# Down projection of a SwiGLU block: pairs of column blocks, seven block products for a third of the k-tile pairs

## The chip, the cores and the metric

The program runs on one core of one Trainium2 chip. The metric is the device time of one execution in microseconds (us), median over runs. The trace comes from one profiled execution of the same program; its time is 1664.86 us and its span 1663.1 us.

TensorE (PE, with its weight load PEld), VectorE (DVE), ScalarE (ACT) and GpSimd (POOL) each work through a queue of their own, in order. Weights come from HBM by DMA, issued from SyncE's queue (SP).

## The reference

One layer of a decoder trunk on 256 tokens of width 2048, in float32: a mixer of three branches, then

```python
h = h + mixed @ w_out
hn = rmsnorm(h, norm_ffn_g)
h = h + (silu(hn @ ffn_w_gate) * (hn @ ffn_w_up)) @ ffn_w_down     # 2048 -> 5632 -> 2048
hp = rmsnorm(h, norm_ple_g)
h = h + (p @ ple_w_proj) * sigmoid(hp @ ple_w_gate)
```

and a final RMSNorm. This case is about the last product of the SwiGLU line, the down projection: (256 x 5632) times (5632 x 2048), added to h.

## The kernel before, in words

**Numbers.** A float32 operand is split into a high part of reduced precision (`hi`, made on ACT by a cast) and the rest (`lo`, made on DVE by a subtraction). One product of a 128 x 128 block of activations (stationary) with a 128 x 512 block of weights (moving) is then three matmuls, hi·hi, lo·hi and hi·lo: `mm2` issues the first two for part 0 and the third for part 1 (L139 to L145).

**Weights.** All weights lie in one array of chunks of 128 x 2048 floats, 1 MB each, in the order of their use. `load` (L102) issues the DMA of a chunk into one of three `raw` tiles; `chunk` (L113) splits it in two steps of 128 x 1024, each into a `whi` and a `wlo` tile out of a ring of three. `split` (L190) does the same for any tile: the cast on ACT is L193, the subtraction on DVE L194.

**Gate and up.** For each of 11 blocks of 512 hidden columns (L1251) the gate and the up product run together over eight pairs of k-tiles, in the order `ORDER`. Five of the pairs use eight block products (two token tiles, two k-tiles, two weight matrices), which is 24 matmuls. The three pairs in `SEVEN` use seven: sums of activation blocks (`SF`, made once, L1212) and sums of weight blocks (`seven`, L1232: two subtractions or additions on DVE, two on POOL at L1240 and L1244, into `tsum`) take part, and the seven products go to four PSUM banks of the pool `mm` (products 2, 4, 3 and 8) and four of the pool `sm` (products 1, 7, 5 and 6, which only these pairs use). After the last such pair the four `sm` banks are combined into four tiles of the pool `b2`, on ACT (`m1`, L1284) and DVE (`u2`, `u3`, `u4`, `v4`); at the end of the block the four `mm` banks are added to them (L219 is the line of the helper `tt`). A gated product `sg` follows (L222, L225), and eight transposes on PE (L1306, into `sm` banks) bring it into `hid`, 44 k-tiles of 128 x 256 (L1307).

**Down.** For each of four blocks of 512 output columns (L1316) `gemm_tm` (L156) runs over the 44 k-tiles, four to a chunk: two token tiles, so eight block products and 24 matmuls to a chunk, accumulated in two of the four `mm` banks. For every chunk the four k-tiles of `hid` are split into `dh` and `dl` in one step of 128 x 1024, so that the whole of `hid` is split four times. The result is added to the residual tiles `h[t, n]` (L1319), and `h_block` (L1157) squares them on ACT, transposes them on PE (L1167, eight transposes into two `sm` banks) and splits the transposes on ACT and DVE (L196, L197, four steps of 128 x 256) as the input of the next product, the PLE gate.

**Order of work.** The program is written in one order, and a scheduler with priorities places the instructions on the engines' queues and gives the buffers of the pools to tiles; once placed, each queue runs in order. Loads, splits of weights and of `hid`, and the combinations at the end of a gate and up block stand in `tc.high_priority()`. The pools have 4 buffers (`mm`, `sm`), 16 (`b2`), 3 (`raw`, `whi`, `wlo`) and 2 (`dh`, `dl`, `tsum`).

Of the kernel before, what the change touches and what calls it, by code (L numbers as in the profile page):

```python
# [38 lines left out]
SEVEN = (0, 1, 2)  # L39

# [34 lines left out]
def trunk(ctx: ExitStack, tc: tile.TileContext, xT, x, pT, wall, vecs, csts, s5b, s5c, gfin, out, dbg=None):  # L75
# [114 lines left out]
    def split(hi, lo, src, gain=None):  # L190
# [4 lines left out]
        else:  # L195
            nc.scalar.activation(out=hi, in_=src, func=AF.Identity if not isinstance(gain, float) else AF.Copy, scale=gain)  # L196
            nc.vector.scalar_tensor_tensor(out=lo, in0=src, scalar=gain, in1=hi.bitcast(F32), op0=ALU.mult, op1=ALU.subtract)  # L197

# [1001 lines left out]
    dn = hid_stack.enter_context(tc.tile_pool(name="dn", bufs=2))  # L1200
# [4 lines left out]

    SF = {}  # L1212
    for u in SEVEN:
        af = t2("af").rearrange("p (a t) -> p a t", a=2)
        sf = t2("sf").rearrange("p (a t) -> p a t", a=4)
        tt(af, hh[:, 2 * u:2 * u + 2, :].bitcast(F32), hl[:, 2 * u:2 * u + 2, :].bitcast(F32), ALU.add)
        tt(sf[:, 0], af[:, 0, TS[1]], af[:, 1, TS[1]], ALU.add)
        tt(sf[:, 1], sf[:, 0], af[:, 0, TS[0]], ALU.subtract)
        tt(sf[:, 2], af[:, 0, TS[0]], af[:, 0, TS[1]], ALU.subtract)
        tt(sf[:, 3], af[:, 1, TS[0]], sf[:, 1], ALU.subtract)  # L1220
        SF[u] = tuple(gu.tile([128, 4, 128], F32R, name=q + "%d" % u) for q in ("sh", "sl"))
        split(*SF[u], sf)

    def tiled(r):

        n = r.shape[1]
        hi = ring.tile([128, 2, 512], F32R, name="whi", tag="whi", bufs=3)[:, 0:n]
        lo = ring.tile([128, 2, 512], F32R, name="wlo", tag="wlo", bufs=3)[:, 0:n]
        split(hi, lo, r)
        return [(hi[:, q], lo[:, q]) for q in range(n)]  # L1230

    def seven():  # L1232

        if not loaded:
            load()
        raw, _ = loaded.pop(0)
# [11 lines left out]
    def A(u, t, k):  # L1248
        return hh[:, 2 * u + k, TS[t]], hl[:, 2 * u + k, TS[t]]

    for b in range(11):  # L1251
        M = {q: pmm() for q in (2, 4, 3, 8)}
        done = set()

        def prods(ops, last):
# [249 lines left out]
```

## Time and profile before

| | |
|---|---|
| time, median of 3 runs | 1666.72 us (1664.29 to 1666.83) |
| the profiled execution | 1664.86 us |
| its span | 1663.1 us, 23487 instructions |
| PE busy | 1641.0 us, 99% of the span |
| DVE busy | 1276.8 us, 77% |
| ACT busy | 908.7 us, 55% |
| POOL busy | 184.8 us, 11% |
| DMA | 313.69 MB, mean 189 GB/s |

Busy times are sums over instructions. Matmuls are pipelined and their ends are modelled, so PE's share says that PE is always occupied, not at what rate; that is read from the starts of its instructions. A wait is booked to what released it. The down projection lies between 1310.1 and 1553.2 us, gate and up between 837 and 1310 us.

### The profile page before, as it was taken

The page shows a single profiled execution, that of the slowest core. Times are in us where ns is not written, and L with a number is a line of the kernel's source. Part 1 is how long each engine was busy: PE and PEld are TensorE (multiplying, and loading weights), DVE is VectorE, ACT ScalarE, POOL GpSimd, SP SyncE. Part 2 cuts the span into 40 slices and gives each one's busy share as a digit, 9 for nine tenths or more (in the row PEclk, how much of TensorE's full clock was granted, in tenths as well). Part 3 has the DMA queues.
Part 4 walks back from the last instruction along what each step waited for, and adds up shares of the span by engine and source line. Part 5 has one row for each costly group of instructions (what it writes and reads, how often), then busy time and mean ns, then how long its engine had stood idle before and what let it go on. Part 6 is the DMA issues. An engine that isn't in the chain of part 4 may idle for free.

```text
span 1663.1 us, 23487 instructions
## 1 busy us (share of the span) xinstructions
PE 1641.0 (99%) x9255; PEld 1380.4 (83%) x9255; DVE 1276.8 (77%) x1590; ACT 908.7 (55%) x1141; POOL 184.8 (11%) x131
## 2 busy tenths in 40 slices
PE   8999999999999999999999999999999999999997
PEld 8999889987888888888877888888888888888886
DVE  6999776969988545575589988888888867666565
ACT  6465566555645434444465555555555656656454
POOL 1100100100000000000032322332233000000000
PEclk9999999999999999999999999999999999999999
DMA  9655544555454444555544555555555655555553
GB/s 363 196 171 175 171 152 183 189 187 190 164 194 159 149 158 152 178 190 194 213 176 181 190 198 203 202 203 192 189 190 190 232 184 197 180 200 185 219 186 118
DMA packets 49455, 313.69 MB, mean 189 GB/s; under 512 B 5824, under 2 KB 9152, under 8 KB 12736
## 3 DMA queue, kind: packets, MB, share of 16 engines
q1 hardware_dynamic: 43488, 304.59, 50.7%
q0 software_dynamic: 3840, 3.15, 1.1%
q10 hardware_dynamic: 2016, 4.46, 0.8%
q8 instruction: 72, 1.18, 0.3%
q14 instruction: 39, 0.32, 0.1%
HBM read 306.93 MB, written 2.10 MB: 186 GB/s over the span
## 4 chain that ended last, share of the span: by engine, by line
PE 94%; DVE 3%; issue 1%; ACT 1%; DMA 1%; POOL 0%; SPq 0%; POOLq 0%; DVEq 0%
PE mm L142 23%; PE mm L143 23%; PE mm L145 23%; PE mm L149 4%; PE mm L152 4%; PE mm L150 4%; PE M L145 2%; PE M L142 2%; PE M L143 2%; DVE wlo L129 1%; DMA raw<-in_wall 1%; PE sm L544 1%; DVE wlo L194 1%; PE sm L1306 0%; PE mm L135 0%
## 5 line engine op out<-in xcount | busy, mean ns | idle before, releaser
L128 ACT CAST whi<-raw 128x1024 fp32r<-128x1024 f32 (+1 forms) x496 | 518.1, 1049 | 552.5 <-PE mm L143 393.4
L129 DVE TENSOR_TENSOR wlo<-raw,whi 128x1024 fp32r<-128x1024 f32 (+1 forms) x496 | 612.2, 1238 | 240.2 <-ACT whi L128 221.4
L143 PE MATMUL mm<-whi,alo 128*128 128x512 f32 x512 | 201.2, 393 | 0.0
L142 PE MATMUL mm<-whi,ahi 128*128 128x512 f32 x512 | 201.0, 393 | 0.0
L142 PE MATMUL mm<-whi,hhi 128*128 128x512 f32 x506 | 198.1, 392 | 0.3 <-DVE m1s L219 0.3
L143 PE MATMUL mm<-whi,hlo 128*128 128x512 f32 x506 | 196.8, 389 | 0.0
L149 PE MATMUL mm<-ahi,whi 128*128 128x256 f32 x576 | 143.3, 286 | 7.8 <-ACT whi L128 7.8
L145 PE MATMUL mm<-wlo,hhi 128*128 128x512 f32 x506 | 146.5, 393 | 0.8 <-DVE wlo L194 0.8
L150 PE MATMUL mm<-alo,whi 128*128 128x256 f32 x576 | 142.7, 285 | 0.0
L145 PE MATMUL mm<-wlo,ahi 128*128 128x512 f32 x512 | 139.2, 392 | 0.0
L142 PE MATMUL mm<-whi,dh 128*128 128x512 f32 x352 | 130.2, 389 | 0.0
L143 PE MATMUL mm<-whi,dl 128*128 128x512 f32 x352 | 130.2, 389 | 0.0
L149 PEld LDWEIGHTS mm<-ahi,whi 128*128 128x128 f32 x576 | 111.4, 194 | 8.8 <-ACT whi L128 8.0
L145 PEld LDWEIGHTS mm<-wlo,hhi 128*128 128x128 f32 x506 | 94.9, 188 | 24.0 <-DVE wlo L194 4.7
L142 PEld LDWEIGHTS mm<-whi,hhi 128*128 128x128 f32 x506 | 95.0, 188 | 23.1 <-issue 3.8
L142 PEld LDWEIGHTS mm<-whi,ahi 128*128 128x128 f32 x512 | 96.1, 188 | 21.2 <-issue 1.2
L143 PEld LDWEIGHTS mm<-whi,alo 128*128 128x128 f32 x512 | 96.1, 188 | 20.9 <-issue 1.2
L145 PEld LDWEIGHTS mm<-wlo,ahi 128*128 128x128 f32 x512 | 95.6, 188 | 20.6 <-issue 0.4
L150 PEld LDWEIGHTS mm<-alo,whi 128*128 128x128 f32 x576 | 111.4, 194 | 0.4 <-issue 0.4
L143 PEld LDWEIGHTS mm<-whi,hlo 128*128 128x128 f32 x506 | 95.0, 188 | 19.6
L1244 POOL TENSOR_TENSOR tsum<-raw,tsum 128x512 f32<-128x512 f32 x33 | 86.8, 2629 | 115.6 <-DVE tsum L219 110.4
L1240 POOL TENSOR_TENSOR tsum<-raw 128x512 f32<-128x512 f32 x33 | 56.0, 1696 | 381.9 <-PE mm L145 177.5
(536 smaller groups left out, 2842.0 us busy)
## 6 DMA issues: line engine op xcount, KB each, us to landing
raw<-in_wall SPq DMA_DIRECT2D x283, 1024.0 KB, 4.8
xrow<-in_x SPq DMA_DIRECT2D x2, 1024.0 KB, 8.7
h<-in_x ACTq DMA_DIRECT2D x8, 256.0 KB, 3.2
xraw<-in_xT SPq DMA_DIRECT2D x3, 512.0 KB, 10.7
ub<-Bh POOLq DMA_DIRECT2D x16, 64.0 KB, 3.8
ub<-uh POOLq DMA_DIRECT2D x16, 64.0 KB, 3.7
gft<-in_gfin ACTq DMA_DIRECT2D x1, 1024.0 KB, 6.0
out_dram<-fin SPq DMA_DIRECT2D x4, 256.0 KB, 3.2
```

The lines of the kernel that those rows point to most:

```text
L128: nc.scalar.copy(out=hi[:, q, :], in_=r)
L129: nc.vector.tensor_tensor(out=lo[:, q, :], in0=r, in1=hi[:, q, :].bitcast(F32), op=ALU.subtract)
L142: nc.tensor.matmul(ps, ah, wh, start=first, stop=False, skip_group_check=skip)
L143: nc.tensor.matmul(ps, al, wh, start=False, stop=False, skip_group_check=skip)
L145: nc.tensor.matmul(ps, ah, wl, start=False, stop=last, skip_group_check=skip)
L149: nc.tensor.matmul(ps, wh, ah, start=first, stop=False, skip_group_check=skip)
L150: nc.tensor.matmul(ps, wh, al, start=False, stop=False, skip_group_check=skip)
L152: nc.tensor.matmul(ps, wl, ah, start=False, stop=last, skip_group_check=skip)
L194: nc.vector.tensor_tensor(out=lo, in0=src, in1=hi.bitcast(F32), op=ALU.subtract)
L544: nc.tensor.matmul(psy[32 * j:32 * j + 32, a * 256:(a + 1) * 256], cc[:, ri, js_, :], G["s5x"][q][ri][:, a, :], start=ri == 0, stop=ri == ...
L1240: nc.gpsimd.tensor_tensor(out=ts_[:, 0], in0=raw[:, 3], in1=raw[:, 0], op=ALU.subtract)
L1244: nc.gpsimd.tensor_tensor(out=ts_[:, 2], in0=raw[:, 1], in1=ts_[:, 1], op=ALU.subtract)
```

## The change

The gate and up loop becomes a function `gemm_pair` that also serves the down projection. There it runs twice, for column blocks 0 and 1 and for 2 and 3, over 22 pairs of k-tiles in their order. A plain pair is one chunk of 24 matmuls as before, now with two k-tiles and two column blocks in it. Seven of the 22 pairs (1, 4, 7, 10, 13, 16, 19) go by seven block products. `hid` is split per pair of k-tiles, in steps of 128 x 512, once for each of the two passes; in the seven pairs four sums of 128 x 128 blocks of `hid` are made on DVE and split as well, in each pass. `dh` and `dl` have three buffers, `dsh` and `dsl` two. After pair 19 the combinations of the `sm` banks are added to the four `h` tiles, and after pair 21 the `mm` banks. Both `h_block`s of a pass follow it. The weight chunks are laid out on the host to fit; their number and size stay. Gate and up computes what it did.

```diff
+DORDER = tuple(range(22))
+DSEVEN = (1, 4, 7, 10, 13, 16, 19)
...
-    def gemm_tm(hi, lo, nkt, split_of=None):
+    def gemm_tm(hi, lo, nkt):
...
-            if split_of is not None:
-                with tc.high_priority():
-                    h_, l_ = (dn.tile([128, 4, T], F32R, name=q, tag=q) for q in ("dh", "dl"))
-                    split(h_, l_, split_of[:, 4 * c:4 * c + 4, :])
-                hi, lo = (lambda k: h_[:, k % 4, :]), (lambda k: l_[:, k % 4, :])
...
+    def sums(sf, a):
+        tt(sf[:, 0], a[:, 0, TS[1]], a[:, 1, TS[1]], ALU.add)
+        tt(sf[:, 1], sf[:, 0], a[:, 0, TS[0]], ALU.subtract)
+        tt(sf[:, 2], a[:, 0, TS[0]], a[:, 0, TS[1]], ALU.subtract)
+        tt(sf[:, 3], a[:, 1, TS[0]], sf[:, 1], ALU.subtract)
...
+    def gemm_pair(A, S, order, by7, pool, prep=None, onto=None):
+        M = {q: pmm() for q in (2, 4, 3, 8)}
...
+        for u in order:
+            last = u == order[-1]
+            if prep is not None:
+                prep(u)
+            if u in by7:
+                if u == by7[0]:
+                    for q in (1, 7, 5, 6):
+                        M[q] = psm("M%d" % q)
+                (b11, b21), (b22, t3), (t1, t2_), (t4_,) = seven(pool)
+                end = u == by7[-1]
+                prods([(1, A(u, 0, 0), b11)], end)
+                prods([(2, A(u, 0, 1), b21)], last)
+                prods([(3, S(u, 3), b22)], last)
+                prods([(7, S(u, 2), t3)], end)
+                prods([(5, S(u, 0), t1)], end)
+                prods([(6, S(u, 1), t2_)], end)
+                prods([(4, A(u, 1, 1), t4_)], last)
+                if end:
+                    with tc.high_priority():
+                        m1, u2, u3, u4, v4 = (t2(q) for q in ("m1s", "u2", "u3", "u4", "v4"))
+                        nc.scalar.copy(out=m1, in_=M[1])
...
+                    res = (m1, u3, u4, v4)
+                    if onto is not None:
+                        for o, r in zip(onto, res):
+                            tt(o, o, r, ALU.add)
+                        res = onto
+            else:
+                b11, b21, b22, b12 = chunk()
+                prods([(2, A(u, 0, 0), b11), (4, A(u, 1, 0), b11), (2, A(u, 0, 1), b21), (4, A(u, 1, 1), b21)], last)
+                prods([(3, A(u, 0, 0), b12), (8, A(u, 1, 0), b12), (3, A(u, 0, 1), b22), (8, A(u, 1, 1), b22)], last)
+        with tc.high_priority():
+            for o, q in zip(res, (2, 4, 3, 8)):
+                tt(o, M[q], o, ALU.add)
+        return res
...
-    dn = hid_stack.enter_context(tc.tile_pool(name="dn", bufs=2))
+    dn = hid_stack.enter_context(tc.tile_pool(name="dn", bufs=3))
...
-    for n in range(4):
-        ps = gemm_tm(None, None, 44, split_of=hid)
-        for t in range(2):
-            nc.vector.tensor_tensor(out=h[t, n], in0=h[t, n], in1=ps[t], op=ALU.add)
-        h_block(n, hT2, "gple", ssq2)
+    dv = {}
+    def down_prep(u):
+        a = hid[:, 2 * u:2 * u + 2, :]
+        with tc.high_priority():
+            dv["a"] = tuple(dn.tile([128, 2, T], F32R, name=q, tag=q) for q in ("dh", "dl"))
+            split(*dv["a"], a)
+            if u in DSEVEN:
+                sf = t2("sf").rearrange("p (a t) -> p a t", a=4)
+                sums(sf, a)
+                dv["s"] = tuple(dn.tile([128, 4, 128], F32R, name=q, tag=q, bufs=2) for q in ("dsh", "dsl"))
+                split(*dv["s"], sf)
+    for n in (0, 2):
+        gemm_pair(lambda u, t, k: tuple(q[:, k, TS[t]] for q in dv["a"]), lambda u, i: tuple(q[:, i, :] for q in dv["s"]),
+                  DORDER, DSEVEN, hid_p, down_prep, (h[0, n], h[1, n], h[0, n + 1], h[1, n + 1]))
+        for m in (n, n + 1):
+            h_block(m, hT2, "gple", ssq2)
```

## Rows read from the trace of the kernel before

**Rows 1.** The page: busy time by engine, the chain that ended last by engine, and the group that counts the down projection's matmuls of one of the three kinds.

```profile
PE 1641.0 (99%) x9255; PEld 1380.4 (83%) x9255; DVE 1276.8 (77%) x1590; ACT 908.7 (55%) x1141; POOL 184.8 (11%) x131
...
PE 94%; DVE 3%; issue 1%; ACT 1%; DMA 1%; POOL 0%; SPq 0%; POOLq 0%; DVEq 0%
...
L142 PE MATMUL mm<-whi,dh 128*128 128x512 f32 x352 | 130.2, 389 | 0.0
```

**Rows 2.** Busy time by stretch: the second block of gate and up, one in the middle of the stage, and the whole of the down projection. Columns: stretch, its length, busy us (instructions) of PE, PEld, DVE, ACT and POOL, granted clock, DMA share, GB/s.

```profile
880.50:924.50 44.00, 43.11 (x191) 34.55 (x190) 41.38 (x43) 25.25 (x30) 10.72 (x6) 1.00 0.53 192
...
1181.20:1224.10 42.90, 42.90 (x193) 34.95 (x191) 37.61 (x41) 24.44 (x30) 13.15 (x6) 1.00 0.54 195
1310.10:1553.20 243.10, 243.10 (x1089) 201.37 (x1088) 169.13 (x157) 143.50 (x162) 0.00 (x0) 1.00 0.54 193
```

**Rows 3.** PE in order of time (start, length): two steps of one chunk in the down projection, each of which ends with four matmuls of part 1.

```profile
1364.63 1.07 PE L145 MATMUL mm<-wlo,dh 128*128 128x512 f32 x4
...
1367.35 1.07 PE L145 MATMUL mm<-wlo,dh 128*128 128x512 f32 x4
```

**Rows 4.** The chain in order of time (start, length): the transposes of two successive column blocks.

```profile
1376.58 0.66 PE sm L1167 x6
...
1437.36 0.66 PE sm L1167 x6
```

**Rows 5.** PE's waits (total us, times, longest): all of the down projection, then the second block of gate and up, then the steady block from 1138.33 us, which the later ones repeat.

```profile
PEld mm L142 <- issue: 0.3, 1, 0.3
...
PEld mm L145 <- DVE wlo L194: 1.4, 2, 0.7
PEld mm L142 <- issue: 0.5, 1, 0.5
PEld M L145 <- DVE wlo L194: 0.3, 1, 0.3
PEld sm L1306 <- DVE sg L222: 0.2, 1, 0.2
...
PEld mm L145 <- DVE wlo L194: 0.4, 1, 0.4
```

**Rows 6.** DVE in order of time in gate and up and at its start: a split of 128 x 1024, a 128 x 512 sum and the next split back to back, and two sums of 128 x 128.

```profile
908.38 1.22 DVE L129 TENSOR_TENSOR wlo<-raw,whi 128x1024 fp32r<-128x1024 f32 x1
909.51 0.69 DVE L219 TENSOR_TENSOR tsum<-raw 128x512 f32<-128x512 f32 x1
910.12 1.22 DVE L129 TENSOR_TENSOR wlo<-raw,whi 128x1024 fp32r<-128x1024 f32 x1
...
842.04 0.48 DVE L219 TENSOR_TENSOR sf<-af 128x128 f32<-128x128 f32 x2
```

**Rows 7.** DVE by shape over seven steady blocks of gate and up, 1010 to 1310 us, 21 pairs by seven products: busy us, mean ns, idle before and its releaser. The last row is the same split over the down projection, where POOL does nothing.

```profile
L129 DVE TENSOR_TENSOR wlo<-raw,whi 128x1024 fp32r<-128x1024 f32 x71 | 93.6, 1327 | 0.0
L194 DVE TENSOR_TENSOR wlo<-raw,whi 128x1024 fp32r<-128x1024 f32 x42 | 57.1, 1399 | 0.0
L194 DVE TENSOR_TENSOR wlo<-tsum,whi 128x1024 fp32r<-128x1024 f32 x21 | 28.2, 1343 | 16.2 <-PE mm L145 16.2
L219 DVE TENSOR_TENSOR raw<-raw 128x512 f32<-128x512 f32 x21 | 14.5, 690 | 16.7 <-POOL tsum L1240 16.7
...
L129 DVE TENSOR_TENSOR wlo<-raw,whi 128x1024 fp32r<-128x1024 f32 x89 | 108.9, 1224 | 64.4 <-ACT whi L128 63.8 <-ACT hid L1307 0.5
```

**Rows 8.** POOL's two sums in a steady block of gate and up (start, length).

```profile
1097.05 1.30 POOL L1240 TENSOR_TENSOR tsum<-raw 128x512 f32<-128x512 f32 x1 [12.93 <-DMA raw<-in_wall]
...
1107.88 2.28 POOL L1240 TENSOR_TENSOR tsum<-raw 128x512 f32<-128x512 f32 x1
1111.69 1.68 POOL L1244 TENSOR_TENSOR tsum<-raw,tsum 128x512 f32<-128x512 f32 x1 [1.53 <-DVE tsum L219]
```

**Rows 9.** ACT by shape over the same seven blocks, and a cast of 128 x 1024 of `hid` over the down projection.

```profile
L193 ACT CAST whi<-tsum 128x1024 fp32r<-128x1024 f32 x21 | 22.1, 1054 | 39.8 <-PE mm L143 39.8
L193 ACT CAST whi<-tsum 128x512 fp32r<-128x512 f32 x21 | 12.9, 615 | 0.7
...
L193 ACT CAST dh<-hid 128x1024 fp32r<-128x1024 f32 x42 | 44.2, 1052 | 0.0
```

**Rows 10.** The boundary between two blocks of gate and up, in order of time: the first of the final additions that wait for the old block's last banks, the last gated product, the transposes, the copies that free their banks, and the first matmul into a bank of `sm`. The new block's matmuls begin at 1267.24 us.

```profile
1268.15 1.28 DVE L219 TENSOR_TENSOR u<-mm,u 128x512 f32<-128x512 f32 x2
...
1275.28 0.74 DVE L222 SCALAR_TENSOR_TENSOR sg<-v,rr,sg 128x512 f32<-128x512 f32 x1
...
1278.69 0.60 PE L1306 MATMUL sm<-ct,sg 128*128 128x128 f32 x4
...
1279.90 1.20 ACT L1307 COPY hid<-sm 128x256 f32<-128x256 f32 x4 [1.20 <-PE sm L1306]
...
1280.49 0.40 PE L142 MATMUL M<-whi,hhi 128*128 128x512 f32 x1
```

**Rows 11.** The boundary between two column blocks of the down projection: the additions to `h`, the first and the last of the four splits of the transposes.

```profile
1370.95 1.28 DVE L1319 TENSOR_TENSOR h<-h,mm 128x512 f32<-128x512 f32 x2 [1.09 <-PE mm L145]
...
1377.46 0.48 DVE L197 SCALAR_TENSOR_TENSOR plo<-sm,vt,phi 128x256 fp32r<-128x256 f32 x1 [1.75 <-ACT phi L196]
...
1382.04 0.48 DVE L197 SCALAR_TENSOR_TENSOR plo<-sm,vt,phi 128x256 fp32r<-128x256 f32 x1
```

**Rows 12.** The end of the down projection: the first matmul of the PLE gate, and the last split of the transposes of column block 3.

```profile
1553.69 0.50 PE L142 MATMUL mm<-whi,phi 128*128 128x512 f32 x1 [0.23 <-ACT whi L128]
...
1564.50 0.48 DVE L197 SCALAR_TENSOR_TENSOR plo<-sm,vt,phi 128x256 fp32r<-128x256 f32 x1
```

More of the change, by code (lines that the diff above doesn't have):

```diff
@@ new lines, in tiled, with seven @@
+    def tiled(r):
+        n = r.shape[1]
+        hi = ring.tile([128, 2, 512], F32R, name="whi", tag="whi", bufs=3)[:, 0:n]
+        lo = ring.tile([128, 2, 512], F32R, name="wlo", tag="wlo", bufs=3)[:, 0:n]
+        split(hi, lo, r)
+        return [(hi[:, q], lo[:, q]) for q in range(n)]
+    def seven(pool):
+        if not loaded:
+            load()
+        raw, _ = loaded.pop(0)
+        with tc.high_priority():
+            ts_ = pool.tile([128, 3, 512], F32, name="tsum", tag="tsum", bufs=2)
+            out_ = [tiled(raw[:, 0:2])]
+            nc.gpsimd.tensor_tensor(out=ts_[:, 0], in0=raw[:, 3], in1=raw[:, 0], op=ALU.subtract)
+            tt(raw[:, 3], raw[:, 2], raw[:, 3], ALU.subtract)
+            out_.append(tiled(raw[:, 2:4]))
+            tt(ts_[:, 1], raw[:, 3], raw[:, 0], ALU.add)
+            nc.gpsimd.tensor_tensor(out=ts_[:, 2], in0=raw[:, 1], in1=ts_[:, 1], op=ALU.subtract)
+            out_ += [tiled(ts_[:, 0:2]), tiled(ts_[:, 2:3])]
+        return out_
@@ new lines, in gemm_pair, with prods @@
+    def gemm_pair(A, S, order, by7, pool, prep=None, onto=None):
+        M = {q: pmm() for q in (2, 4, 3, 8)}
+        done = set()
+        def prods(ops, last):
+            n_ = {q: max(i for i, o in enumerate(ops) if o[0] == q) for q in {o[0] for o in ops}}
+            for part in range(2):
+                for i, (q, a, w) in enumerate(ops):
+                    mm2(M[q], *a, *w, part, q not in done, last and part == 1 and i == n_[q], True)
+                    if part == 0:
+                        done.add(q)
+        for u in order:
[19 more added lines that the diff above has]
+                        nc.scalar.copy(out=m1, in_=M[1])
+                        tt(u2, M[6], m1, ALU.add)
+                        tt(u3, M[7], u2, ALU.add)
+                        tt(u4, M[5], u2, ALU.add)
+                        tt(v4, M[5], u3, ALU.add)
+                    res = (m1, u3, u4, v4)
[11 more added lines that the diff above has]
+        return res
@@ L1203, in trunk @@
     hh, hl = hT
[L1212 to L1236, printed above, removed]
-        with tc.high_priority():
-            ts_ = gu.tile([128, 3, 512], F32, name="tsum", tag="tsum", bufs=2)
-            out_ = [tiled(raw[:, 0:2])]
-            nc.gpsimd.tensor_tensor(out=ts_[:, 0], in0=raw[:, 3], in1=raw[:, 0], op=ALU.subtract)
-            tt(raw[:, 3], raw[:, 2], raw[:, 3], ALU.subtract)
-            out_.append(tiled(raw[:, 2:4]))
-            tt(ts_[:, 1], raw[:, 3], raw[:, 0], ALU.add)
-            nc.gpsimd.tensor_tensor(out=ts_[:, 2], in0=raw[:, 1], in1=ts_[:, 1], op=ALU.subtract)
-            out_ += [tiled(ts_[:, 0:2]), tiled(ts_[:, 2:3])]
-        return out_
+    SF = {u: sums_of(hh, hl, u, gu) for u in SEVEN}
     def A(u, t, k):
@@ L1251, in trunk @@
     for b in range(11):
[L1252 to L1295 removed]
+        c11, c21, c12, c22 = gemm_pair(A, lambda u, i: tuple(q[:, i, :] for q in SF[u]), ORDER, SEVEN, hid_p)
         sg = []
[L1297 removed]
+        for t, (g_, u_) in enumerate(((c11, c12), (c21, c22))):
             s_ = t2("sg")
```

59 lines of the change are left out of this document (17 added, 42 removed).

## The prediction

> **What bounds the kernel now.** I read the page first. PE is busy for 99% of the span and holds 94% of the chain that ended last, at the full clock [rows 1, 2]: time is gained where PE has less to issue, and lost where it has to wait. Then the table by stretches, since a mean over the run hides that the down projection is unlike its neighbour: there PE is busy in all of its 243.1 us, DVE in 169.1 (70%), ACT in 143.5 (59%), POOL not at all [rows 2]. Then PE's starts, because its lengths are modelled. Two like steps of 12 matmuls start 1367.35 - 1364.63 = 2.72 us apart, so one costs 0.2267 us [rows 3]. Three kinds of 352 are 1056 matmuls [rows 1], 239.4 us. From one column block to the next are 1437.36 - 1376.58 = 60.78 us [rows 4], less 264 x 0.2267 = 59.84: 0.94 us for eight transposes. 239.4 + 4 x 0.94 = 243.2 is the whole stage, so PE loses nothing there; its only wait in the list is 0.3 us [rows 5].
>
> Gate and up already works as the down projection will. Its steady block takes 42.9 us for 183 matmuls (41.5) and eight transposes (0.94): about 0.45 us are lost, and the list names a wait of 0.4 us for a `wlo` of DVE [rows 2, 5]. Its second block, where DVE is busy in 41.4 of 44 us (94%) in place of 37.6 of 42.9 (88%), loses 2.4 us by its four waits [rows 2, 5].
>
> **The matmuls.** Each of the seven pairs issues 21 matmuls in place of 24. Two passes of seven: 42 matmuls less, 42 x 0.2267 = 9.5 us, all on the path. PE's work becomes 507 x 0.2267 + 1.9 = 116.8 us in a pass, 233.6 in both.
>
> On this rate a page of the Trainium skill, "TensorE: Matmul & The Clock Gate" (Part 1), gives 215.7 ns for a warm matmul of 512 columns. The trace disagrees, with 226.7 ns [rows 3]; by the page the saving would be 9.1 us.
>
> **DVE.** From one start to the next a split of 128 x 1024 takes 1.13 us, an operation of 128 x 512 0.61, one of 128 x 128 0.20 [rows 6]; a split of a transpose 0.48 [rows 11]. A plain pair costs two weight splits and one of `hid` half as large as before: 2 x 1.13 + 0.61 = 2.87. A pair by seven: three large weight splits and a small one, 4.00; two sums for `seven`, 1.22; `dl`, 0.61; four small sums, 0.80; `dsl`, 0.61; together 7.24, against 21 x 0.2267 = 4.76 of PE. A pass has 15 x 2.87 = 43.1, 7 x 7.24 = 50.7, 12 combinations and additions to `h`, 7.3, and eight splits of transposes, 3.8: 104.9 us, beside 116.8 of PE. That leaves 11.9, or 1.70 us to each pair by seven for what POOL does to DVE.
>
> The trace shows two such costs. In 21 pairs by seven the 134 large splits take 93.6 + 57.1 + 28.2 = 178.9 us, where 1.224 each (POOL idle) would be 164.0: 14.9 more, 0.71 a pair. And DVE waits 16.7 us for POOL's first sum, 0.80 a pair [rows 7]. With the first DVE comes to 109.9 of 116.8 (94%), with both to 115.5 (99%). So PE remains the bound, barely, and the deficit of a pair by seven, 7.24 + 0.71 - 4.76 = 3.2 us, must be covered by what lies ready: the ring of three holds two steps ahead, 5.4 us of PE in a plain pair, and the two plain pairs that follow give back 2 x (5.44 - 2.87) = 5.1. Covered, with little over.
>
> What PE loses is bounded by the steady block (0.4 us to three pairs by seven, 0.13 each) and the second (2.4, 0.8 each) [rows 5]: 1.9 to 11.2 us over 14 pairs. Nothing below zero, as PE has no idle time to give. DVE's share is that of the second block, but pairs by seven are three apart here and mostly two there, so twice the recovery; I take 0.25, nearer the steady block: 3.5 us.
>
> **ACT** comes to 15 x (2 x 1.05 + 0.62) + 7 x (3 x 1.05 + 3 x 0.62) = 76 us of casts in a pass [rows 9], and some 7 for `m1`, squares and transposes: 71% of PE. The DMAs are as many and as large, in 4% less time; no cost. The halved splitting of `hid` gains nothing by itself, since DVE and ACT were covered; it pays for the sums.
>
> **Start of the down projection.** Pair 1 wants a bank of `sm` 5.4 us after the start. In gate and up the gated products leave DVE 8.8 us after a block's start, the transposes follow at 11.5, and the first matmul into `sm` comes 13.3 after it [rows 10]; there the first pair by seven is third, here second. If the banks go to the transposes first, pair 1 waits 13.3 - 5.4 = 7.9 us, less its three products that need no such bank, 2.0: 5.9 at most. If they go to pair 1, the transposes wait, which only pairs 20 and 21 need: zero. The scheduler sees banks free and matmuls ready, so I take 0.5.
>
> **Between the passes** all four `mm` banks are in use. Products 2 and 4 end half a chunk (2.72 us) early, which covers their additions (1.28, [rows 11]), and 3 and 8 are wanted 2.72 us later: zero; the block boundary of gate and up, with the same banks, shows about 0.5 us [rows 5]. But two `h_block`s now use four `sm` banks at once. Before, four splits come 1.53 us apart, from 6.5 to 11.1 us after the additions begin [rows 11]; eight would end at 17.2. The next pass wants its fourth `sm` bank at 5.4 + 5 x 0.68 + 1.9 (transposes) = 10.7. So 0 to 6.5 us. In the pass's last two plain pairs DVE has slack to be ready for it; I take 1.
>
> **At the end** eight splits in place of four stand between the last addition and the PLE gate, which reads column block 2 only in its third chunk, 10.9 us on. Before, the last split came 1564.50 - 1553.69 = 10.8 us after the gate's first matmul, and PE had waited 0.23 [rows 12]. Eight cost 0 to 4 x 1.53 = 6 us; proj2 (5.4 us) and 16 transposes lie between, so zero.
>
> **Sum**, against the profiled execution: 1664.86 - 9.5 + 3.5 + 0.5 + 1.0 = 1660.4 us. The median shown lies 1.9 above that execution and its lowest run 0.6 below; I leave the forecast there.
>
> **Rivals.** *The gain in full.* The scheduler hides all but 1.5 us. For it: the steady block's 0.13 us a pair. Against: DVE at 94% in place of 88%. 1664.9 - 9.5 + 1.5 = 1656.9.
>
> *The banks take it back.* At the start and between the passes half of the 5.9 + 6.5 us are paid: 1664.9 - 9.5 + 3.5 + 6.2 = 1665.1, no change. For it: in rows 10 `sm` matmuls come right behind the copies that free the banks. Against: PE has other matmuls to place before.
>
> *POOL's sums make DVE the bound.* Place: the 14 pairs by seven. If POOL's 1.30 and 1.68 us [rows 8] shut DVE out for all their length, each pair costs 2.98 in place of the 1.70 that is free, and PE waits (2.98 - 1.70) x 14 = 17.9: 1664.9 - 9.5 + 17.9 + 1.5 = 1674.8. From 1.70 us a pair on DVE costs PE time, from (9.5 - 1.5) / 14 + 1.70 = 2.27 the kernel is slower than before. For it: POOL's sum itself stretches from 1.30 to 2.28 beside DVE [rows 8], and 0.71 + 0.80 is already 1.51, with fuller queues here. Against: the 0.71 is measured with DVE nearly as full.
>
> The Trainium skill, "SBUF — State Buffer" (Who interferes with whom), has the rule: a DVE instruction with two SBUF inputs contends with a GpSimd instruction that reads SBUF, and whoever comes second blocks fully. By that rule the rival holds in full; the trace agrees that both are stretched, with 0.71 us a pair on DVE.
>
> **How the numbers follow.** About 0.2% (3.3 us) can be told from no change. Forecast, 1658.5 to 1662.5: 0.44. Gain in full, below: 0.15. Banks, up to 1667: 0.21. DVE as the bound, above: 0.20. Faster by over 3.3 us (below 1661.6) is the gain in full and most of the forecast, 0.49; slower (above 1668.2) the last case, 0.20; the rest 0.31. The range, 1655.3 (nothing lost) to 1670, leaves out the upper half of the last case and little else. The forecast's own range is 1658.5 to 1662.5.
>
> **What would show it.** In the down projection 1014 matmuls of 512 columns in a stretch of 237 to 240 us; 12 matmuls still 2.72 us apart in plain pairs; PE's waits there for `wlo` of L194 or L129, some 3 to 4 us in sum; DVE busy above 90% of it; large splits at 1.3 to 1.4 us mean. A wait of PE for `plo` or for `hid` at the boundaries above 2 us speaks for the banks; PE's waits above 8 us behind DVE, and DVE without idle time, for the third rival. I am wrong if the time leaves 1655.3 to 1670, or if PE's waits lie elsewhere.

## The result and the profile after

The changed kernel takes 1685.27 us (median of 5 runs, 1684.04 to 1687.28) against 1666.5 us (1664.29 to 1666.83), a ratio of 1.0118 with a 95% interval of 1.0103 to 1.0133. It is slower by 1.2%, where 1660.4 us and a range up to 1670 stood in the prediction. Its profiled span is 1685.2 us, 22.1 more than before. That execution took 1686.98 us, 1.7 above its median, and the one profiled before lies 1.6 below its own: by the medians the change costs 18.8 us.

The page after, in the lines that answer to [rows 1], and of the 40 slices those of PE and its clock:

```profile
PE 1647.3 (98%) x9213; PEld 1380.5 (82%) x9213; DVE 1338.8 (79%) x1732; ACT 920.4 (55%) x1185; POOL 241.8 (14%) x159
...
PE   8999999999999999999999999999999899899997
...
PEclk9999999999999999999999999999999999899999
...
PE 91%; DVE 5%; issue 1%; ACT 1%; DMA 1%; POOL 0%; SPq 0%; POOLq 0%; ACTq 0%; DVEq 0%
```

The 42 matmuls are gone (9255 - 9213), and yet PE is busy for longer. Late in the span two slices show an 8 for PE, and the clock line dips in the second of them. The table by stretches says where they lie (columns as in [rows 2]): gate and up, the start of the down projection, its first pass, the boundary between the passes, its second pass, its end.

```profile
837.75:1318.40 480.65, 474.92 (x2096) 385.33 (x2095) 423.79 (x461) 271.12 (x327) 144.18 (x68) 0.99 0.53 191
1318.40:1345.00 26.60, 19.19 (x71) 13.30 (x71) 25.10 (x53) 12.42 (x19) 10.58 (x3) 0.87 0.29 102
1345.00:1425.00 80.00, 80.00 (x353) 65.94 (x352) 67.36 (x71) 50.26 (x62) 16.75 (x9) 1.00 0.55 197
1425.00:1480.00 55.00, 49.23 (x202) 39.00 (x201) 52.82 (x87) 32.07 (x48) 11.31 (x5) 0.91 0.48 171
1480.00:1553.00 73.00, 73.00 (x323) 60.45 (x323) 61.94 (x65) 46.81 (x57) 14.46 (x10) 1.00 0.52 189
1553.00:1576.00 23.00, 23.00 (x107) 19.12 (x107) 22.15 (x26) 13.46 (x18) 1.79 (x1) 1.00 0.63 233
```

Inside a pass PE is busy all the time at the full clock, and DVE in 84% of it (67.36 of 80). Three pairs there, one of them by seven, take 15.64 us, which is 69 x 0.2267: nothing is lost. The loss sits in 26.6 us at the start (7.4 without PE, clock 0.87), in 55 us between the passes (5.8 without PE, clock 0.91; DVE 96%), and in gate and up, which computes what it did. PE's waits in those places, from 870 to 1000 us, from 1316 to 1345 and from 1425 to 1480:

```profile
PE mm L148 <- DVE wlo L192: 5.0, 5, 2.0
...
PE sm L1324 <- DVE sg L324: 2.0, 1, 2.0
PE mm L145 <- issue: 1.8, 1, 1.8
PE mm L145 <- DVE u L321: 1.4, 2, 0.9
PE mm L148 <- DVE wlo L192: 1.2, 1, 1.2
...
PE mm L145 <- ACT dsh L191: 2.7, 1, 2.7
PE sm L1269 <- DVE h L321: 2.2, 1, 2.2
PE mm L145 <- ACT whi L191: 0.6, 1, 0.6
PE M L145 <- DVE plo L195: 0.4, 1, 0.4
```

In the last four, only the 0.4 us for `plo` is a wait for an `sm` bank. The others are for operands and sums that DVE and ACT had not yet made, above all `dsh`, the split sums of `hid` that pair 1 of the second pass reads. At the start banks have a larger part. The 1.4 us for `u` are waits for `mm` banks that DVE's last additions of gate and up had not yet read. The 2.0 us for `sg` pass at the transposes of gate and up's last block, which stand in PE's queue just ahead of pair 1's first product into `sm` (1331.40 and 1332.19 us). Where pair 1 of the first pass is plain (e1_eight, e4_from4 and e14_pair1_second below), PE waits for neither at the start.

**The ledger.** Four marks cut a trace into five parts that add up to the span: the starts of the first and of the last matmul on `hhi` (the high part of gate and up's input), of the first on `dh`, and of the first of the PLE gate. The starts are read to 0.1 us, so a part can be 0.1 off. By them gate and up took 474.6 us before and 481.9 after (+7.3), the gap to the down projection 0.3 and 2.2 (+1.9), the down projection 243.6 and 254.8 (+11.2), the end 109.4 and 109.8 (+0.4); gate and up began at 835.2 and 836.5 (+1.3, with no edit ahead of it; from 160 to 180 us the granted clock is 0.91 in the trace after and 1.00 in the one before). The down projection should have shrunk by 9.5 to 234.1, so it lost 20.7. PE in order of time (start, length), the same step of four matmuls in the two passes:

```profile
1375.14 1.07 PE L148 MATMUL mm<-wlo,dh 128*128 128x512 f32 x4
...
1503.18 1.07 PE L148 MATMUL mm<-wlo,dh 128*128 128x512 f32 x4
```

They are 128.04 us apart and hold 116.8 us of work: 11.2 of the 20.7 are lost between the passes, 9.5 at the start. DVE is busy in 113.6 us of this stretch:

```profile
1375.14:1503.18 128.04, 122.27 (x525) 99.46 (x523) 113.62 (x149) 78.73 (x106) 25.10 (x15) 0.96 0.50 181
```

**What stands in front.** DVE in order of time, in the second block of gate and up, before and then after:

```profile
896.07 0.69 DVE L194 TENSOR_TENSOR wlo<-tsum,whi 128x512 fp32r<-128x512 f32 x1
896.67 2.33 DVE L194 TENSOR_TENSOR dl<-hid,dh 128x1024 fp32r<-128x1024 f32 x1
...
897.29 0.69 DVE L192 TENSOR_TENSOR dl<-hid,dh 128x512 fp32r<-128x512 f32 x1
897.90 1.75 DVE L192 TENSOR_TENSOR wlo<-tsum,whi 128x512 fp32r<-128x512 f32 x1
899.57 0.68 DVE L192 TENSOR_TENSOR dl<-hid,dh 128x512 fp32r<-128x512 f32 x1
```

These `dl` are the first splits of `hid` for the down projection, 420 us before it begins. They have high priority, their input is there, and the pool of `dn` gives them a buffer, so the scheduler puts them in front of weight splits that PE waits for. The pool has three buffers, and three such pairs of `dh` and `dl` go into gate and up's first blocks. The kernel before has such splits too, but there the first stands behind the small `wlo` of the same pair, and after the change ahead of it. What that costs is more than the 0.61 us of the `dl`: the `wlo` now falls beside POOL's second sum (897.46 to 899.11 us) and takes 1.75 us in place of 0.69, and PE waits 1.94 us for it, where it had waited 0.28.

At the end of gate and up and then between the passes, pieces of the chain (start, length):

```profile
1319.23 0.69 DVE tsum L321
1319.91 0.60 DVE m1s L321
...
1434.65 0.60 DVE h L321
...
1438.15 4.78 DMA raw<-in_wall
1443.07 3.83 POOL tsum L239
...
1455.30 2.10 DVE sf L321 x10
1457.40 1.11 DVE wlo L192
...
1458.86 0.88 DVE sf L321 x4
...
1461.32 1.14 DVE wlo L192
...
1463.29 0.63 ACT dsh L191
1463.96 0.80 PE mm L145
```

The first two lie in the gap: a sum of weights for pair 1 stands ahead of the addition into `m1s`, which reads the `mm` bank that the down projection's first product needs (it begins at 1320.61 us). In the table below the gap is 2.2 us where the early splits stand in gate and up and pair 1 of the first pass goes by seven, and 0.3 where that pair is plain: the +1.9 belongs to pair 1.

Between the passes runs of ten and four small sums stand in DVE's queue ahead of the splits that pair 1 needs. These are the sums for several pairs at once: outside gate and up the pool of 16 tiles that they come from has room for them.

### The profile page after: what moved, and what is told of

Same layout as the page of the kernel before. It is cut to its first block, busy times and chain, and to the rows that moved or that the text cites. A ratio compares the mean times of both kernels' runs of the same rounds, so it can differ in the third digit from the quotient of the medians.

```text
span 1685.2 us, 23700 instructions
## 1 busy us (share of the span) xinstructions
PE 1647.3 (98%) x9213; PEld 1380.5 (82%) x9213; DVE 1338.8 (79%) x1732; ACT 920.4 (55%) x1185; POOL 241.8 (14%) x159
## 4 chain that ended last, share of the span: by engine, by line
PE 91%; DVE 5%; issue 1%; ACT 1%; DMA 1%; POOL 0%; SPq 0%; POOLq 0%; ACTq 0%; DVEq 0%
PE mm L145 22%; PE mm L146 22%; PE mm L148 21%; PE mm L152 4%; PE mm L155 4%; PE mm L153 4%; PE M L148 2%; PE M L145 2%; PE M L146 2%; DVE wlo L132 1%; DVE wlo L192 1%; PE sm L646 1%; DVE sf L321 1%; DMA raw<-in_wall 1%; DVE sg L324 0%
## 5 line engine op out<-in xcount | busy, mean ns | idle before, releaser
L131 ACT CAST whi<-raw 128x1024 fp32r<-128x1024 f32 (+1 forms) x468 | 487.4, 1048 | 482.6 <-PE mm L146 314.2
L132 DVE TENSOR_TENSOR wlo<-raw,whi 128x1024 fp32r<-128x1024 f32 (+1 forms) x468 | 586.6, 1259 | 181.0 <-ACT whi L131 166.0
L239 POOL TENSOR_TENSOR tsum<-raw 128x512 f32<-128x512 f32 x47 | 84.3, 1794 | 528.7 <-DMA raw<-in_wall 291.1
L191 ACT CAST whi<-raw 128x1024 fp32r<-128x1024 f32 x94 | 99.0, 1053 | 78.3 <-PE mm L146 66.5
L243 POOL TENSOR_TENSOR tsum<-raw,tsum 128x512 f32<-128x512 f32 x47 | 115.3, 2454 | 166.6 <-DVE tsum L321 161.4
L192 DVE TENSOR_TENSOR wlo<-raw,whi 128x1024 fp32r<-128x1024 f32 x94 | 124.2, 1341 | 10.2 <-PE mm L148 10.1
L191 ACT CAST whi<-tsum 128x1024 fp32r<-128x1024 f32 x94 | 77.1, 836 | 80.2 <-PE mm L146 65.2
L192 DVE TENSOR_TENSOR wlo<-tsum,whi 128x1024 fp32r<-128x1024 f32 x94 | 97.9, 1051 | 26.6 <-PE mm L148 23.8
L148 PEld LDWEIGHTS mm<-wlo,ahi 128*128 128x128 f32 x512 | 95.6, 188 | 20.7 <-issue 0.4
```

The source lines that it names most:

```text
L131: nc.scalar.copy(out=hi[:, q, :], in_=r)
L132: nc.vector.tensor_tensor(out=lo[:, q, :], in0=r, in1=hi[:, q, :].bitcast(F32), op=ALU.subtract)
L148: nc.tensor.matmul(ps, ah, wl, start=False, stop=last, skip_group_check=skip)
L191: nc.scalar.copy(out=hi, in_=src)
L192: nc.vector.tensor_tensor(out=lo, in0=src, in1=hi.bitcast(F32), op=ALU.subtract)
L239: nc.gpsimd.tensor_tensor(out=ts_[:, 0], in0=raw[:, 3], in1=raw[:, 0], op=ALU.subtract)
```

## The experiments

Two theories. *The early preparations* (H in the expectations): work of high priority is put far ahead of its use wherever a pool has a free buffer, and stands in front of urgent work. *The boundaries* (B): a pass cannot begin with a pair by seven so soon, because DVE and ACT still owe the end of the stage before. Most kernels ran once, and the ten runs of e5_all spread over 5.5 us, so 1 or 2 us between the times of single runs tell little. Marks in us, one profiled execution each; the down projection's ideal is 243.6 - 0.2267 x 3 for each pair by seven:

| kernel | gate/up | gap | down (ideal) | end | span |
|---|---|---|---|---|---|
| before | 474.6 | 0.3 | 243.6 | 109.4 | 1663.1 |
| after | 481.9 | 2.2 | 254.8 (234.1) | 109.8 | 1685.2 |
| e1_eight | 481.6 | 0.3 | 243.1 (243.6) | 109.2 | 1668.7 |
| e2_sf1 | 480.4 | 2.2 | 247.0 (234.1) | 109.8 | 1676.1 |
| e3_dnlate | 473.4 | 3.4 | 253.0 (234.1) | 109.8 | 1674.3 |
| e4_from4 | 478.6 | 0.3 | 238.7 (235.4) | 109.8 | 1663.8 |
| e5_all | 474.2 | 1.6 | 239.7 (235.4) | 109.8 | 1660.2 |
| e6_dn_from4 | 473.5 | 1.6 | 239.5 (235.4) | 109.8 | 1660.8 |
| e7_seven_from4 | 474.2 | 1.5 | 244.5 (234.1) | 109.9 | 1664.1 |
| e8_ptlate | 480.5 | 2.2 | 254.1 (234.1) | 110.4 | 1684.0 |
| e9_defer | 474.1 | 1.6 | 240.2 (235.4) | 109.8 | 1662.4 |
| e10_from3 | 476.3 | 1.5 | 238.5 (235.4) | 110.3 | 1663.6 |
| e11_before_dn | 473.3 | 1.5 | 243.7 | 109.3 | 1664.3 |
| e12_two | 474.0 | 1.6 | 241.3 (235.4) | 110.1 | 1663.2 |
| e13_early_two | 477.4 | 2.2 | 256.4 (234.1) | 110.2 | 1682.7 |
| e14_pair1_second | 481.6 | 0.3 | 248.2 (234.8) | 109.8 | 1674.1 |
| e15_late_sf1 | 474.0 | 3.4 | 248.3 (234.1) | 109.9 | 1671.7 |

**No pair by seven** (e1_eight). What do the new passes cost by themselves?

```diff
-DSEVEN = (1, 4, 7, 10, 13, 16, 19)
+DSEVEN = ()
```

> The changed kernel, with all 22 pairs of the down projection by eight block products (no sums, no sm banks, no combinations), the splitting per pair and the two passes kept. Marks of the changed kernel: gate and up 481.9 us from its first matmul to its last against 474.6 before; down projection with its start 254.8 against 243.6, of which the steady part loses nothing, the start about 9.5 and the place between the passes about 11.2. Theory H (high-priority preparations of hid are placed too early and in front of urgent work): gate and up stays near 482, because the three early splits of hid stay; the starts lose 0 to 2 us each; down about 244 to 247. Theory B (the banks and combinations at the two boundaries): gate and up stays where it is for another reason, the two boundaries lose nothing, down 243 to 244. Either way 1670 to 1676 us; a down projection above 250 would say that the four mm banks per pass are the cause.

1670.5 us. The down projection by pairs of column blocks and halved splits costs nothing: 243.1 us. Gate and up is as long as after the change, so its loss does not come from pairs by seven.

**Sums of `hid` in one buffer** (e2_sf1), so that they can't run ahead:

```diff
+    sfp = hid_stack.enter_context(tc.tile_pool(name="sfp", bufs=1))
...
-                sf = t2("sf").rearrange("p (a t) -> p a t", a=4)
+                sf = sfp.tile([128, 4, 128], F32, name="dsf", tag="dsf")
```

> The changed kernel with one buffer of its own for the small sums of hid (before, any free tile of the pool of 16), so that they can be made for one pair at a time. Theory H: at the start and between the passes the runs of 9 to 12 sums on DVE disappear; each boundary gives back 3 to 6 us; down 244 to 249 in place of 254.8; gate and up unchanged at 482; total 1675 to 1681. Theory B: down stays within 2 us of 254.8, total 1683 to 1687.

1677.85 us; the down projection gets 7.8 us of its 20.7 back. Runs of sums do stand in the way, and are the smaller part. Part of the 7.8 is the clock: from 1318 to 1345 us it is granted at 1.00 here and at 0.87 in the changed kernel.

**The pool of early splits opened behind gate and up** (e3_dnlate), so that none can be put there:

```diff
-    dn = hid_stack.enter_context(tc.tile_pool(name="dn", bufs=3))
...
     gu_stack.close()
+    dn = hid_stack.enter_context(tc.tile_pool(name="dn", bufs=3))
```

> The changed kernel with the pool of dh, dl, dsh and dsl opened behind gate and up, in the memory that its sums free, so that no split of hid can be made in the first blocks of gate and up. Theory H: gate and up goes from 482 back to 475 or less (473 if even the early loss of the kernel before goes), down unchanged within 3 us of 254.8; total 1676 to 1679. If gate and up stays at 482, its loss has nothing to do with the early splits of hid. Theory B says nothing of gate and up; a shorter down (by over 4 us) would speak against both.

1676.14 us. Gate and up falls to 473.4, below the kernel before. Its waits for `wlo` from 870 to 1000 us, against 5.0 after:

```profile
PE mm L148 <- DVE wlo L192: 0.6, 2, 0.4
```

Two of the splits stand in DVE's queue ahead of the addition into `m1s` now, and the gap grows by 1.2 us.

**The first pair by seven is pair 4** (e4_from4, the fourth kernel):

```diff
-DSEVEN = (1, 4, 7, 10, 13, 16, 19)
+DSEVEN = (4, 7, 10, 13, 16, 19)
```

> The changed kernel with six pairs by seven (4, 7, 10, 13, 16, 19): the first comes 21.8 us after the start of a pass in place of 5.4; six matmuls more, 1.4 us. Theory B: both boundaries have the time they need, the start and the place between the passes lose 0 to 3 us each in place of 9.5 and 11.2; down 237 to 241. Theory H: the sums are still made early and in a row in front of other work; each boundary still loses over 5 us, down 248 to 254. Gate and up 482 by both; total 1667 to 1672 by B, 1679 to 1685 by H.

1665.59 us: the down projection falls by 16.1 us although PE has 1.4 us more to do, and loses 3.3. Between the passes (as above, 1425 to 1480 us):

```profile
1425.00:1480.00 55.00, 54.34 (x248) 44.42 (x247) 54.92 (x85) 35.43 (x53) 8.33 (x4) 1.00 0.51 188
```

DVE is fuller than it was (54.92 of 55 against 52.82), and PE loses 0.7 in place of 5.8. So it is not DVE's share that decides here, but what PE wants of it at that time.

**All three together** (e5_all): the late pool, the sums in one buffer and the first pair by seven at 4.

> The changed kernel with all three edits: the pool of dh and dsh behind gate and up, one buffer for the small sums, six pairs by seven from pair 4 on. If the three causes add up as seen alone: gate and up 473.4 us (as with the late pool), a gap of 0.3, the down projection 236 to 238.5 (238.7 from pair 4 on; up to 3.3 us above its 235.4 of pure PE work, of which the sums' buffer gives back some): span 1654 to 1657, time 1656 to 1659, faster than both kernels by 0.3 to 0.6%. If the late pool only moves the loss to the start of the down projection, the gap and down together stay 3 us longer: 1659 to 1662.

1663.56 us over 10 runs against 1665.85 over 13, a ratio of 0.9991 (0.9981 to 1.0). The cures do not add up fully: the late pool leaves a gap of 1.6, where the fourth kernel had 0.3, and PE waits 1.9 us for `h` between the passes.

The same without the one buffer for the sums (e6_dn_from4):

> The same without the one buffer for the sums (late pool, six pairs from pair 4 on). If the run of sums matters only where it falls on the boundaries' crowded DVE, then with the first pair by seven late it matters little: within 1.5 us of the kernel with all three, down 237 to 239. If the sums in a row are a cause of their own, down is 240 or more.

1662.56 us in one run, down projection 239.5: with pair 1 out of the way the one buffer is worth nothing that a single run can tell.

**Seven pairs, the first still pair 4** (e7_seven_from4):

```diff
-DSEVEN = (4, 7, 10, 13, 16, 19)
+DSEVEN = (4, 6, 9, 11, 14, 16, 19)
```

> Late pool, one buffer for sums, and again seven pairs by seven, now 4, 6, 9, 11, 14, 16 and 19, closer together. PE's work is 1.4 us less than with six. By the sum of DVE's work two pairs two apart take 7.24 + 0.7 + 2.87 = 10.8 us of DVE to 10.2 of PE, so each such place overdraws 0.6 and the third pair pays it back: if the first position alone was wrong, down is 235 to 237.5; if DVE's density decides, 238 to 242.

1665.85 us, down projection 244.5: 1.4 us less of work for PE and 4.8 us longer. Where two pairs by seven lie two apart, PE waits, 3.2 us in the first pass from 1340 to 1425 us, all for casts and splits of weights. Three apart covers a pair by seven, two apart does not.

**The PLE input split behind the down projection** (e8_ptlate). The chain at the start runs through the load of `praw` and its split (L1331 in the changed kernel):

```diff
-    split(ph_, pl_, pr_)
...
+    split(ph_, pl_, pr_)
```

> The changed kernel with the splitting of p (the input of the PLE projection) issued behind both passes in place of at the start of the first. In the chain of the changed kernel ACT stands 1.9 us before it for the DMA, and 2.6 us of that chain are this DMA. If the wait is on the path, the down projection is 2 to 4 us shorter (251 to 253) and the start shows no such link; if the start is limited by DVE's queue anyway, within 1 us of 254.8. Gate and up 482, total 1681 to 1687.

1685.76 us, down projection 254.1. The load of 2.58 us stood in the chain, and 0.7 us came back: what stood beside it was as late.

**Transposes of the first pass deferred** (e9_defer) into the second, in the version with all three edits:

```diff
+    def prep2(u):
+        if u == 2:
+            for m in (0, 1):
+                h_block(m, hT2, "gple", ssq2)
+        down_prep(u)
```

> The version with all three edits (pool late, sums in one buffer, seven products from pair 4), and the squares and transposes of blocks 0 and 1 placed behind two pairs of the second pass. Boundary theory: the 1.9 us that PE waited between the passes at the transposes of h go; down projection 237 to 238 us in place of 239.7, time 1661.5 to 1663. If that wait only moves to the next thing that is late (the first weight splits of the second pass, or an sm bank), it stays at 239 to 240 and the time at 1663 to 1664.

1663.36 us over 10 runs against 1665.88 over 13, a ratio of 0.9987 (0.9978 to 0.9997); the down projection is no shorter. PE's wait between the passes in the version with all three, then in this one:

```profile
PE sm L1269 <- DVE h L321: 1.9, 1, 1.9
...
PE mm L145 <- DVE h L321: 2.0, 1, 2.0
```

The same additions to `h` on DVE that held the transposes now hold a product of the next pass, which needs the `mm` bank that they read: the wait moved. Six pairs by seven save 8.2 us of matmuls, and 2.5 of them reach the time, which is less than the 0.2% that was taken as the least that can be told.

**The first pair by seven is pair 3** (e10_from3), in the version with deferred transposes:

```diff
-DSEVEN = (4, 7, 10, 13, 16, 19)
+DSEVEN = (3, 6, 9, 12, 15, 18)
```

> As the one before with the six pairs by seven one place earlier (3, 6, 9, 12, 15, 18). The same products, so the ideal is the same. Boundary theory: how early the first pair by seven comes decides; moved from pair 4 to pair 3 it has one plain pair less to fill the ring, so 1 to 4 us more, down projection 239 to 242. If only pair 1 was too early, the same 237 to 238.

1665.36 us. The expected loss did not come: 238.5, shorter than from pair 4. One plain pair less at the start does no harm that shows; pair 2 as the first was not tried. The last pair by seven moved as well, from 19 to 18, and the 2.0 us for `h` between the passes are gone: one more plain pair ahead of the boundary helps, as far as one run tells. Gate and up came out 2.2 us longer, with 2.9 us of waits for `wlo` from 870 to 1310 us, although the pool is late; why, was not followed.

**The kernel before with its pool late** (e11_before_dn):

```diff
-    dn = hid_stack.enter_context(tc.tile_pool(name="dn", bufs=2))
...
     gu_stack.close()
+    dn = hid_stack.enter_context(tc.tile_pool(name="dn", bufs=2))
```

> The kernel before, with its pool for the early splits of hid opened only behind gate and up. Theory of the early splits: its gate and up has them too, two of 128 x 1024 in the second block, so 474.6 falls to about 473.4 (as with the late pool after the change), and the gap ahead of the down projection grows by 1 to 3 us, since the splits then stand there: time within 2 us of before. If gate and up stays at 474.6, the 1.2 us were not theirs.

1666.03 us. The kernel before paid 1.3 us in gate and up for its own early splits, and loses 1.2 in the gap without them.

**Two buffers in place of three**, first in the version with deferred transposes (e12_two):

```diff
     gu_stack.close()
-    dn = hid_stack.enter_context(tc.tile_pool(name="dn", bufs=3))
+    dn = hid_stack.enter_context(tc.tile_pool(name="dn", bufs=2))
```

> As the one with the deferred transposes, but the pool of early splits has its place of old, ahead of gate and up, and two buffers in place of three. Theory of the early splits: two of them, of half the size before, cost gate and up less than three: 474 to 478 in place of 478.6 to 481.9, and the gap goes back to 0.3. If what is lost is not by their number, gate and up stays at 478 to 482.

1665.0 us. The expectation describes another kernel than the one that ran: the pool stood in its late place here, with two buffers. So it tells only that two buffers cost the down projection 1.1 us against three (PE waits 2.6 us for `dl`). The changed kernel with the pool in its early place and two buffers (e13_early_two):

```diff
-    dn = hid_stack.enter_context(tc.tile_pool(name="dn", bufs=3))
+    dn = hid_stack.enter_context(tc.tile_pool(name="dn", bufs=2))
```

> The changed kernel with two buffers in place of three in the pool of early splits, which stays ahead of gate and up. If the loss of gate and up goes by the number of early splits, two of half the old size cost it less than three: 474 to 478 us for gate and up in place of 481.9. If it goes by where the first ones are put (second block, in front of weight splits), two cost as much as three: 479 to 482.

1684.49 us, down projection 256.4. Gate and up 477.4, its waits for `wlo` 2.6 in place of 5.0: the loss goes by the number of early splits, as far as one run tells. The fourth kernel, with three, has 478.6 us and so hardly more, but its waits for `wlo` are 5.0 us like those of the changed kernel; what it is spared is the fall of the clock that follows them there (last section).

**Pair 1 by seven in the second pass alone** (e14_pair1_second):

```diff
     for n in (0, 2):
+        dv["seven"] = DSEVEN[1:] if n == 0 else DSEVEN
```

> The changed kernel with pair 1 by eight products in the first pass and by seven in the second: 1.4 us more of TensorE's work. If each start of a pass pays for its own pair 1, the 9.5 us lost at the start of the down projection go and the 11.2 between the passes stay: down projection 254.8 - 9.5 + 1.4 = 246 to 248. If the loss between the passes only hands on what was late at the start, both go: 239 to 242.

1675.94 us, down projection 248.2, 1.5 above the 246.7 that was expected if each start pays for its own pair 1. The start has one wait left, 2.3 us for a `whi`, as in the fourth kernel (2.2), but here the clock falls behind it (last section), which makes up for most of the 1.5. Between the passes PE's waits are those of the changed kernel: 2.7 us for `dsh`, 2.1 for `h`, 0.6 for `whi` and 0.4 for `plo`.

**Late pool and one buffer for the sums, pair 1 by seven** (e15_late_sf1): the edits of the second and the third kernel.

> The changed kernel with the pool of early splits opened behind gate and up and the small sums in one buffer, pair 1 still by seven. If pool and sums add up: gate and up 473 to 474.5, down projection 245 to 247, gap 2 to 3.5, span 1665 to 1668, which leaves 8 to 10 us of loss at the boundaries to pair 1 itself. If the sums matter only where early splits also stand in gate and up, the down projection stays at 251 to 253.

1673.48 us. Down projection 248.3, a little above the first expectation and below the second: pool late and sums in order, pair 1 at the starts still loses 14.2 us, against 4.3 in the version with all three, so 9.9 us are its own, the clock's fall in its company included. One wait at the start, 0.9 us for `hid`, is plainly for an `sm` bank, which ACT's copy of the transposes had still to read.

## Why the prediction was wrong

- *The matmuls, -9.5:* right. 42 fewer, each still 0.2267 us apart in the steady pairs.
- *PE's stalls in the 14 pairs, +3.5 (1.9 to 11.2):* too high. Between the boundaries nothing is lost (80.00 of 80.00). DVE is at 84% there, not 94%. The upper bound was also too high by itself: its 2.4 us in the second block are waits of the weight load, and by the block's length (44.0 against 41.5 + 0.94) only 1.6 are lost.
- *The failed step* is the price of the two boundaries, +0.5 and +1.0: both went by the banks of `sm` alone, and DVE was taken to have slack to be ready for them. Behind that slack stands the 94%: 109.9 us of DVE's work set against the 116.8 of a whole pass. The amount was about right (113.6 us were measured from pass to pass), but the work is not spread like that. The 12 combinations, the splits of the transposes and the first pair by seven fall on one boundary, and there the cover that the sum counted on, two plain pairs on either side, is missing: before pair 1 there is one. The prediction itself named the mean over a run as what hides a stage, and then took a mean over a pass.
- *Start, +0.5 (0 to 5.9):* 9.5 measured; *between the passes, +1.0 (0 to 6.5):* 11.2. Places right, sizes wrong, and both above their bounds. The bounds priced one resource, the banks of `sm`. Between the passes 0.4 us are booked to such a bank, and what PE waits for is the preparation of pair 1. At the start the 2.0 us at the transposes ahead of pair 1's first `sm` product are in the order that the prediction's bound described (whether for want of a bank or by the scheduler's choice no row shows), and 1.4 us are for `mm` banks, which it did not price there; the rest is splits of weights and the clock. Leaving pair 1 out gives 16.1 us back; with the pool late and the sums in order it still costs 9.9, and the rest goes with the sums of later pairs that stand ahead of it, the early pool and the clock, which these runs do not separate.
- *Gate and up, taken at nothing:* +7.3, and +1.9 in the gap. The prediction took code that computes the same for code that runs the same. The pool's third buffer let one more early split into its first blocks, and the early splits now stand ahead of weight splits that are wanted at once: from 870 to 1000 us PE waits 5.0 us for `wlo` where it had waited 1.3, and about 3.4 more go by the clock (last section). That the loss goes with the pool's place was shown, and with its size by one run; that it is the order on DVE is read from the trace. The gap's 1.9 are pair 1's, not the pool's.
- *The end, 0:* +0.4. Right.
- *A term that was missing:* PE at half its clock after the stalls. Of 55 us between the passes 9% are 5.0 us, of 26.6 at the start 13% are 3.5; these are upper estimates, since PE also stood idle in part of that time.

Of the rivals, the gain in full was ruled out by the boundaries, though it was nearest for the steady pairs. The banks had the right places, but between the passes the wrong resource, and at the start only a part of the loss. DVE as the bound by POOL's sums, which gave a slower kernel, was wrong in its place: the pairs between the boundaries don't pay.

What stays open: how much of the boundary between the passes is POOL's slow sum (3.83 us in the chain above) and how much DVE's order alone; no run took POOL out. The 4.3 us that the best versions still lose at the boundaries were not taken apart.

## What to carry to other kernels

A deficit that the steady state covers must be checked where a stage begins and ends: add up, for each boundary alone, what the engines still owe and what the first steps want by when, and start the costly kind of step only behind some plain ones. Where a scheduler places work by priority, a pool's size and the place where it is opened limit how far ahead work goes; a buffer more, or a stage that makes more small preparations, changes the order of code that nobody touched. So compare every stage of the two traces, not only the edited one.

## What was not expected of the hardware

**The clock.** Between the passes the granted clock fell right behind the stalls. The table by stretches of 4 us:

```profile
1446.00:1450.00 4.00, 1.84 (x9) 1.23 (x8) 3.08 (x5) 2.56 (x6) 0.88 (x1) 0.95 0.38 160
1450.00:1454.00 4.00, 4.00 (x16) 3.20 (x15) 4.00 (x6) 1.11 (x5) 1.28 (x1) 0.63 0.59 184
1454.00:1458.00 4.00, 4.00 (x23) 3.34 (x22) 4.00 (x16) 3.65 (x9) 0.00 (x0) 1.00 0.19 78
1458.00:1462.00 4.00, 2.35 (x8) 0.99 (x7) 4.00 (x12) 3.05 (x5) 0.00 (x0) 1.00 0.59 180
1462.00:1466.00 4.00, 2.04 (x5) 1.47 (x6) 4.00 (x11) 2.54 (x4) 2.32 (x1) 0.65 0.20 82
1466.00:1470.00 4.00, 4.00 (x11) 3.13 (x10) 4.00 (x7) 0.78 (x2) 0.00 (x0) 0.50 0.02 4
```

PE is busy in 1.84 of 4 us and then runs on at 0.63; it is busy in 2.35 and 2.04 and then runs a whole stretch at 0.50, the lower of its two levels (1.2 of 2.4 GHz). Its matmuls then start 0.43 us apart:

```profile
1466.69 0.63 PE L145 MATMUL mm<-whi,dh 128*128 128x512 f32 x1
1467.12 0.63 PE L146 MATMUL mm<-whi,dl 128*128 128x512 f32 x1
1467.54 0.63 PE L145 MATMUL mm<-whi,dh 128*128 128x512 f32 x1
```

So these stalls cost nearly twice what the list of waits shows: 5.8 us without PE and about 5.0 by the clock. But a stall does not always bring this. A single wait of 2.0 us in the version with deferred transposes leaves the clock at 1.00; one of 2.3 us in e14_pair1_second is followed by 0.59 (first two lines below). In gate and up the same wait is followed by 0.57 in the changed kernel (next two) and by 1.00 in the fourth (last two):

```profile
1340.00:1344.00 4.00, 2.18 (x10) 1.49 (x8) 2.61 (x4) 0.23 (x1) 3.73 (x1) 1.00 0.25 104
1344.00:1348.00 4.00, 3.56 (x9) 2.78 (x10) 2.88 (x4) 4.00 (x6) 0.00 (x0) 0.59 0.67 262
...
896.00:900.00 4.00, 2.06 (x8) 1.35 (x8) 3.96 (x6) 2.32 (x4) 1.65 (x1) 1.00 0.50 209
900.00:904.00 4.00, 4.00 (x12) 3.10 (x12) 3.66 (x4) 1.12 (x2) 0.00 (x0) 0.57 0.12 16
...
896.00:900.00 4.00, 2.07 (x9) 1.37 (x9) 3.96 (x5) 2.34 (x4) 1.65 (x1) 1.00 0.49 205
900.00:904.00 4.00, 4.00 (x19) 3.32 (x18) 3.59 (x4) 1.91 (x3) 0.00 (x0) 1.00 0.08 33
```

One such fall takes 1.7 us here (0.43 of a stretch of 4 us). The changed kernel has two in gate and up (the second stretch, 948 to 952 us, has 0.60), about 3.4 us of its 7.3; the fourth kernel has none and is 3.3 us shorter there. What decides it no run shows, so a few us between single runs can be the clock alone. The Trainium skill, "TensorE: Matmul & The Clock Gate" (Part 1), gives 426.7 ns between matmuls of 512 columns at the lower level, and the trace agrees with 0.43 us between the passes.

**POOL beside a full DVE.** POOL's first sum of a pair, in order of time: in pair 4 of the first pass, made while pair 1 is computed, in a pair between the boundaries, and in pair 1 of the second pass:

```profile
1333.16 4.28 POOL L239 TENSOR_TENSOR tsum<-raw 128x512 f32<-128x512 f32 x1 [11.89 <-DMA raw<-in_wall]
...
1389.39 1.30 POOL L239 TENSOR_TENSOR tsum<-raw 128x512 f32<-128x512 f32 x1 [8.94 <-DMA raw<-in_wall]
...
1443.07 3.82 POOL L239 TENSOR_TENSOR tsum<-raw 128x512 f32<-128x512 f32 x1 [15.31 <-DMA raw<-in_wall]
```

The same sum takes 1.29 to 2.07 us in the first pass between the boundaries and about three times the 1.30 at them, where DVE is busy in 94 and 96% of the time. Pair 1 of the first pass had its sum earlier, at 1314.38 us, in 1.87 us. The rule that the prediction weighed, of the Trainium skill, "SBUF — State Buffer" (Who interferes with whom), blocks whichever of the two comes second. The trace agrees in that both are stretched. Here it is mostly POOL, by 3.0 us and 2.5, and which instruction of DVE held it no row shows. In gate and up's second block it is DVE: the `wlo` that starts at 897.90 us, 0.44 behind POOL's sum, ends 0.54 us after it, about the time that it takes when it comes alone (0.61 from start to start).
